# Two matmul orders and one square: the low halves last in the down projection, a later turn of half of h, and one square on VectorE

## The chip, the cores and the metric

The kernel runs on one core of one Trainium2 chip. The metric is the device time of one execution in microseconds (us). The time before is the median of three runs, 918.59 us (918.48 to 919.51). The profile is of one further execution, which took 918.14 us by the same clock and whose trace spans 916.4 us from the first to the last instruction. The core's engines are PE (TensorE: matmuls, and PEld for its weight loads), DVE (VectorE), ACT (ScalarE), POOL (GpSimd) and SP (SyncE, which issues most of the DMAs).

## The reference

A bidirectional encoder trunk of two layers over 256 tokens of width 1024, all in 32-bit floats. Cut to the sub-layers that matter here, each layer does:

```python
mixed = jax.nn.sigmoid(gate_a) * branch_a + jax.nn.sigmoid(gate_b) * branch_b
h = h + rms_norm(mixed @ w_out, g_mix_post)                       # stage "wout"

gate, up = jnp.split(rms_norm(h, g_ffn_pre) @ w_ffn_in, 2, axis=-1)   # stage "ffnin"
h = h + rms_norm((jax.nn.silu(gate) * up) @ w_ffn_out, g_ffn_post)    # down projection, "ffnout"

e = p_i @ w_ple_proj
h = h + rms_norm(jax.nn.sigmoid(h @ w_ple_gate) * e, g_ple_post)      # stage "ple"

def rms_norm(x, g):
    y = x * lax.rsqrt(jnp.mean(x * x, axis=-1, keepdims=True) + EPS)
    return y * g
```

Ahead of them in each layer stand the combined input projection, gated linear attention (branch A) and grouped-query attention (branch B). The hidden width of the feed-forward block is 2816, so its down projection multiplies 256 x 2816 by 2816 x 1024.

## The kernel before, in words

**Precision.** Each 32-bit operand of a matmul is kept as two tiles in a reduced 32-bit format: a high part (a cast by ACT) and a low part (the value minus the high part, by DVE). `split` (L133) issues this pair. A product then takes three matmuls: high x high, high x low and low x high. `mm3` (L107) issues the three for one 128 x 128 block of tokens and one 128 x 512 block of weights; `passes` (L113) does the same for several blocks, with one of the three kinds last. Weights come by DMA as 1 MB units, four blocks of 128 x 512 each, into a `raw` tile, and are split into `wh` and `wl`.

**Halves and turns.** The 256 tokens are two halves of 128 rows, `hf` 0 and 1. PE wants its left operand with the features on the partitions, so each result is turned by PE: `transpose_in` (L443) issues four 128 x 128 transposes into one accumulator (`aux`) and splits that into the high and low tiles of a `Split`. `turn_in` (L520) does so for the 1024 columns of one half, as two groups of four transposes.

**The order on PE.** Matmuls are issued in the order of the program text. Side work such as the transposes waits as a `Task`, a generator that yields how many ticks it wants to wait; `tick()` is called after about every six matmuls of 512 columns, and a task whose ticks are over is run there. `WAIT_H` (three ticks for half 0, five for half 1, both layers) is the wait of the turn of h behind the down projection; `WAIT_IN[1][1]` (six ticks) that of half 1 behind `wout` in the second layer (numbered 1; the first is numbered 0). A planner then puts each engine's instructions in order: of those that are ready by its estimate, the one of the highest priority; `tc.high_priority(AHEAD)` raises that of the norms and of the splits behind the transposes. On the chip the order is fixed, and an instruction that waits holds up all behind it on its engine.

**Down projection.** `out_step(n, hf, w)` (L1589) takes one unit of `w_ffn_out` (256 hidden features, `kk` 0 and 1, times two column halves `j`) for one half of the tokens: 12 matmuls, by `mm3` for each `kk` and `j`, into the two accumulators `o[hf][j]`. Eight of the 11 units are done between the blocks of the up projection (part `ffnin` in the tile names), and the last three in `ffnout`: all three for half 0, then all three for half 1. Behind each half follow `post_norm_add` and `turn_in(hT, ...)`:

```python
        for hf in range(2):
            for n, w in zip(outs, us):
                out_step(n, hf, w)
            ...
            post_norm_add(o[hf], gpost, hf)
            turn_in(hT, h[:, hf, :], hf, WAIT_H[l][hf])
```

`by_half(hT, after_gate, ...)` then multiplies half 0 of hT, and after it half 1, by `w_ple_gate`; the accumulators keep the name of the part in which they were made, so those of the down projection are `acc_0ffnin` and `acc_1ffnin` to the end.

**Norms.** `row_rstd` (L477) squares the parts of a row block with ACT at L495 (sums in the columns of `ss`), adds the two sums and the epsilon on POOL (L507) and takes the power -1/2 there (L511). All of its squares are written to one scratch tile, `junk`, from its first column. `post_norm_add` then multiplies by the gain (L126, DVE) and adds to h (L580, DVE, two pieces of 512 columns). `pre_norm` (L530) squares the new h, and scales it on DVE (L515, two pieces) into the tile that is turned next. `after_out` (L1507) calls both behind each half of `wout`.

Of the kernel before, what the change touches and what calls it, by code (L numbers as in the profile page):

```python
# [14 lines left out]
ALU = mybir.AluOpType  # L15
# [11 lines left out]
WAIT, WAIT_FIRST, WAIT_FFN, WAIT_BLOCK = 6, 4, 4, 6  # L27

WAIT_NEXT, WAIT_IN, WAIT_H = (7, 9), ((6, 9), (6, 6)), ((3, 5), (3, 5))
# [13 lines left out]
OUT = (0, 1, 2, 3, 4, 5, 10, 6, 7, 8, 9)  # L43
# [16 lines left out]
def trunk_kernel(ctx: ExitStack, tc: tile.TileContext, a: dict, out: bass.AP):  # L60
# [7 lines left out]
    nc = tc.nc  # L68
# [20 lines left out]
    def mid(dt=F32):  # L89
        return b4p.tile([P, 1024], dt, tag="mid", name=nm("mid"))  # L90

    def acc():
        return accp.tile([P, 512], F32, tag="acc", name=nm("acc"))

    def aux():
        return accp.tile([P, 512], F32, tag="acc", name=nm("aux"))

    def t512():
        return smp.tile([P, 512], F32, tag="t512", name=nm("t512"), bufs=5)

    def small(n, tag, bufs=None):
        return smp.tile([P, n], F32, tag=tag, name=nm(tag), **({"bufs": bufs} if bufs else {}))

    def mm(o, lhsT, rhs, start, stop):
        return nc.tensor.matmul(o, lhsT, rhs, start=start, stop=stop)  # L105

    def mm3(o, l, r, start, stop):  # L107
        (lh, ll), (rh, rl) = l, r
        mm(o, lh, rh, start, False)
        mm(o, lh, rl, False, False)  # L110
        mm(o, ll, rh, False, stop)
# [24 lines left out]
    h = cp.tile([P, 2, D], F32, tag="h", name="h")  # L136
# [69 lines left out]
    for l in range(DEPTH):  # L206
        w = a["w_in"][l]
# [12 lines left out]
        w = a["w_ffn_in"][l]  # L220
# [151 lines left out]
    def gain(v, t, n):  # L372
        nc.sync.dma_start(t[:, :n], v.unsqueeze(0).broadcast_to([P, n]))
        return t[:, :n]
# [24 lines left out]
    def tick():  # L399

        for t in list(tasks):
            t.left -= 1
            if t.left <= 0:
                t.go()
# [38 lines left out]
    def transpose_in(sp, src, k, n, hf, plain=None):  # L443

        ps = aux()
        for i in range(n):
            nc.tensor.transpose(ps[:, i * P : (i + 1) * P], src[:, i * P : (i + 1) * P], ident)
        with tc.high_priority(AHEAD):
            sp.put(ps[:, : n * P], k, n, hf * P, P)
        if plain is not None:  # L450
            nc.scalar.copy(plain, ps[:, : n * P])
# [3 lines left out]
    def in_turn():  # L455

        return tc.issue_after(last_pow[0].ins) if last_pow[0] is not None else nullcontext()
# [16 lines left out]

    last_square = [None]

    def row_rstd(parts, behind=None):  # L477

        ss, r, junk = small(3, "ss"), small(1, "rstd"), mid() if parts[0].shape[-1] > 512 else t512()
        for j, src in enumerate(parts):
            n = src.shape[-1]
            if j == 2 and behind is not None:
                last_square[0] = nc.vector.scalar_tensor_tensor(
                    out=junk[:, :n], in0=src, scalar=1.0 / 1024.0, in1=src, op0=ALU.mult, op1=ALU.mult,
                    accum_out=ss[:, j : j + 1],
                )
                nc.vector.tensor_scalar(  # L490
                    out=r, in0=ss[:, 2:3], scalar1=ss[:, 0:1], scalar2=None, op0=ALU.add
                )
            else:
                with tc.issue_after(behind.ins) if j and behind is not None else nullcontext():
                    last_square[0] = nc.scalar.activation(  # L495
                        junk[:, :n], src, AF.Square, scale=1.0 / 32.0, accum_out=ss[:, j : j + 1]
                    )
            if len(parts) == 3 and j == 1:

                with in_turn():  # L500
                    last_pow[0] = nc.gpsimd.tensor_scalar(
                        out=ss[:, 0:1], in0=ss[:, 0:1], scalar1=ss[:, 1:2], scalar2=EPS if behind is not None else 0.0,
                        op0=ALU.add, op1=ALU.add,
                    )
        with in_turn():
            if behind is None or len(parts) == 2:
                nc.gpsimd.tensor_scalar(  # L507
                    out=r, in0=ss[:, 0:1], scalar1=ss[:, len(parts) - 1 : len(parts)], scalar2=EPS,
                    op0=ALU.add, op1=ALU.add,
                )  # L510
        last_pow[0] = nc.gpsimd.tensor_tensor(out=r, in0=r, in1=neghalf[:, 0:1], op=ALU.pow)  # L511
        return r

    def scale_gain(out, in0, r, g):
        nc.vector.scalar_tensor_tensor(out=out, in0=in0, scalar=r, in1=g, op0=ALU.mult, op1=ALU.mult)  # L515

    def halves(t):
        return [t[:, j * 512 : (j + 1) * 512] for j in range(2)]

    def turn_in(sp, x, hf, wait, plain=None):  # L520


        def turn():
            yield wait
            for j, y in enumerate(halves(x)):
                transpose_in(sp, y, 4 * j, 4, hf, plain and plain[j])

        sp.makers[hf].append(Task(turn(), part[0]))

    def pre_norm(g, hf, sp, wait=WAIT, plain=None):  # L530

        x, gs = halves(h[:, hf, :]), halves(g)
        with tc.high_priority(AHEAD):
            xn = mid()
            r = row_rstd(x)
            for j, y in enumerate(halves(xn)):
                scale_gain(y, x[j], r, gs[j])

        turn_in(sp, xn, hf, wait, plain)
# [26 lines left out]
    def post_norm_add(parts, g, hf, behind=None, store=None, squared=None):  # L566

        with tc.high_priority(AHEAD):
            yt = mid()
            r = row_rstd(squared or parts, behind)  # L570
            cuts, c = [], 0
            for src in parts:
                cuts.append(slice(c, c + src.shape[-1]))
                c += src.shape[-1]
            for j, (src, c) in enumerate(zip(parts, cuts)):
                with tc.issue_after(last_square[0].ins) if j and len(parts) == 3 and behind is not None else nullcontext():
                    vmul(yt[:, c], src, g[:, c])
            for c in cuts if store else (slice(0, 512), slice(512, 1024)):
                x = h[:, hf, c]
                added = nc.vector.scalar_tensor_tensor(  # L580
                    out=x, in0=yt[:, c], scalar=r, in1=x, op0=ALU.mult, op1=ALU.add
                )
                if store:
                    store(c)
        return added
# [138 lines left out]
    def project_t(sp):  # L724

        o = [acc(), acc()]
        for kh in range(2):
            wmode(o, sp, kh * 4, ws.take(), kh == 0, kh == 1)
            ws.done()
        return o  # L730

    def project(sp):

        o = [acc(), acc()]
        for kh in range(2):
            w = ws.take()
            for hf in range(2):
                amode(o[hf], sp, hf, kh * 4, w, kh == 0, kh == 1)
            ws.done()
        return o  # L740
# [81 lines left out]
    ss = [small(2, "ss") for _ in range(2)]  # L822
# [179 lines left out]
    for l in range(DEPTH):  # L1002
# [104 lines left out]
        o = {}  # L1107
# [139 lines left out]
        for x in range(2):  # L1247
            o = project_t(uT)
            for i in range(2):
                dst = qk[:, x, 2 * i : 2 * i + 2, :]  # L1250
                src = o[i].rearrange("p (h t) -> p h t", t=T)
# [142 lines left out]
        for j in range(2):  # L1394
            o = project(uT)
# [107 lines left out]
        gpre = gain(a["g_ffn_pre"][l], mid(), D)  # L1503
        u2 = Split()
        plain = [halves(mid()) for _ in range(2)]

        def after_out(hf, o):  # L1507
            post_norm_add(o, gpost, hf)
            pre_norm(gpre, hf, u2, WAIT_IN[l][hf], plain[hf])

        if l == 0:
            embedding = embed(l, 3)
# [7 lines left out]
        hid = Split()  # L1520
# [11 lines left out]
        for hf in range(2):  # L1532
            ws.lend = hf == 1
            for b in range(2):
                o = acc()
# [51 lines left out]
        o = []  # L1587

        def out_step(n, hf, w):  # L1589
            if not o:  # L1590
                o.extend([acc(), acc()] for _ in range(2))
            wh, wl = (t[:, :2048].rearrange("p (k c) -> p k c", c=512) for t in w)
            for kk in range(2):
                k = 2 * n + kk
                hid.need(hf, k)
                for j in range(2):
                    mm3(
                        o[hf][j], hid.tok(k, hf), (wh[:, 2 * kk + j, :], wl[:, 2 * kk + j, :]),
                        n == OUT[0] and kk == 0, n == OUT[-1] and kk == 1,
                    )  # L1600
                tick()

        outs = list(OUT)
        steps, pairs, seven_ = chain.from_iterable(block(b) for b in PLAIN), list(PAIRS), None
        for x in FFN:
# [3 lines left out]
            if x == "o":  # L1609
                n, w = outs.pop(0), ws.take()  # L1610
# [16 lines left out]
        hT = Split()  # L1627
# [3 lines that stand above are left out]
                if hf == 1:  # L1631
                    ws.done()
            post_norm_add(o[hf], gpost, hf)

            turn_in(hT, h[:, hf, :], hf, WAIT_H[l][hf])


        e = big().rearrange("p (s c) -> p s c", s=2)
# [89 lines left out]
```

## Time and profile before

| what | value |
|---|---|
| time, median of 3 runs | 918.59 us (918.48 to 919.51) |
| time of the profiled execution | 918.14 us |
| its span, first to last instruction | 916.4 us |
| granted TensorE clock, mean | 0.999 |
| ACT busy in the span | 64% |
| DMA, mean over the span | 189 GB/s |

A profile here is one execution. Its page gives the busy time of each engine, a chain of work followed back from the last instruction, and groups of instructions by source line. Further views of the same trace used below are the list of waits (who waited for whom, with the total, the number and the longest in us), the chain in order of time (start, duration, what, how many), the timeline (start, duration, engine, line, operation, tile written and tiles read, count, and in brackets the idle time before it), and the instructions of one source line (durations as least/median/greatest in ns). A matmul's duration in the timeline overlaps the next one's; the distance between starts is what it costs PE.

### The profile page before, as it was taken

To read this page: it belongs to the slowest core of one execution; us is meant where nothing else is said; L and a number is where in the kernel's file an instruction comes from. 1 tells how busy PE (TensorE), PEld (TensorE's weight loads), DVE (VectorE), ACT (ScalarE), POOL (GpSimd) and SP (SyncE) were. 2 spreads that over 40 slices of the span, in tenths; PEclk is the share of its full clock that TensorE was granted. 3 is DMA by queue.
4 is the path that set the end of the run, shared out by engine and by line. 5 is a ranking of instruction groups with operands and counts; after the bars stand their busy time and mean duration, and the time that the engine had idled before them with its cause. 6 is when DMAs were issued, how large, how long until landed. Compare 5 with 4: busy or idle time off the path is not lost.

```text
span 916.4 us, 12439 instructions
## 1 busy us (share of the span) xinstructions
PE 908.1 (99%) x4674; PEld 776.5 (85%) x4674; DVE 786.2 (86%) x1007; ACT 584.1 (64%) x970; POOL 102.4 (11%) x156
## 2 busy tenths in 40 slices
PE   9999999999999999999999999999999999999996
PEld 8998888888888888888899988888888888888886
DVE  6989989987669998999779789799876899989885
ACT  6688767564567565566676687675645766565563
POOL 3700221300100000000334001110001000000000
PEclk9999999999999999999999999999999999999999
DMA  8664445657385555657576424455574756555361
GB/s 283 199 202 136 139 138 190 213 186 255 107 302 181 200 199 199 232 168 247 178 260 222 147 92 139 138 184 184 184 252 134 269 172 211 222 172 222 122 246 46
DMA packets 88680, 173.45 MB, mean 189 GB/s; under 512 B 3422, under 2 KB 26470, under 8 KB 88108
## 3 DMA queue, kind: packets, MB, share of 16 engines
q1 hardware_dynamic: 88316, 172.27, 55.3%
q8 instruction: 36, 0.59, 0.3%
q10 hardware_dynamic: 304, 0.40, 0.1%
q14 instruction: 24, 0.20, 0.1%
HBM read 169.50 MB, written 3.15 MB: 188 GB/s over the span
## 4 chain that ended last, share of the span: by engine, by line
PE 96%; DVE 2%; issue 1%; ACT 0%; POOLq 0%; POOL 0%; DVEq 0%; ACTq 0%
PE acc_1ffnin L121 12%; PE acc_0ffnin L121 11%; PE acc_1gate L121 7%; PE acc_0gate L121 7%; PE acc_1ffnin L105 7%; PE acc_0ffnin L105 6%; PE acc_1rq L121 3%; PE acc_0gqk L121 3%; PE acc_1gqk L121 3%; PE acc_1wout L121 2%; PE acc_0wout L121 2%; PE acc_0ple L121 2%; PE acc_1gg L121 2%; PE acc_0gg L121 2%; PE acc_1v L121 2%; PE acc_0v L121 2%
## 5 line engine op out<-in xcount | busy, mean ns | idle before, releaser
L105 PE MATMUL acc_0ffnin<-wh_0ffnin,big_0ffnin 128*128 128x512 f32 x176 | 56.9, 393 | 0.1
L105 PE MATMUL acc_1ffnin<-wh_1ffnin,big_1ffnin 128*128 128x512 f32 x176 | 56.8, 392 | 0.0
L133 ACT CAST wh_1ffnin<-raw_1ffnin 128x1024 fp32r<-128x1024 f32 x38 | 38.5, 1049 | 26.8 <-DMA raw_1ffnin<-in_w_ffn_out_dram 8.6
L133 ACT CAST wh_0ffnin<-raw_0ffnin 128x1024 fp32r<-128x1024 f32 x38 | 38.2, 1048 | 24.8 <-PE acc_0ffnin L121 7.1
L133 DVE TENSOR_TENSOR wl_1ffnin<-raw_1ffnin,wh_1ffnin 128x1024 fp32r<-128x1024 f32 x38 | 44.9, 1220 | 8.7 <-ACT wh_1ffnin L133 8.6
L133 DVE TENSOR_TENSOR wl_0ffnin<-raw_0ffnin,wh_0ffnin 128x1024 fp32r<-128x1024 f32 x38 | 44.7, 1220 | 8.3 <-ACT wh_0ffnin L133 8.1
L121 PE MATMUL acc_1ffnin<-wh_1ffnin,big_1wout 128*128 128x512 f32 x168 | 42.5, 393 | 0.0
L121 PE MATMUL acc_0ffnin<-wh_0ffnin,big_0wout 128*128 128x512 f32 x168 | 42.5, 393 | 0.0
L105 PEld LDWEIGHTS acc_0ffnin<-wh_0ffnin,big_0ffnin 128*128 128x128 f32 x176 | 33.0, 188 | 7.2 <-DVE big_0ffnin L133 0.5
L105 PEld LDWEIGHTS acc_1ffnin<-wh_1ffnin,big_1ffnin 128*128 128x128 f32 x176 | 33.1, 188 | 6.7
L133 DVE TENSOR_TENSOR wl_1ffnin<-lent_1ffnin,wh_1ffnin 128x1024 fp32r<-128x1024 f32 x30 | 35.8, 1218 | 1.8 <-ACT wh_1ffnin L133 1.7
L133 DVE TENSOR_TENSOR wl_0ffnin<-lent_0ffnin,wh_0ffnin 128x1024 fp32r<-128x1024 f32 x30 | 35.8, 1217 | 1.7 <-ACT wh_0ffnin L133 1.7
L121 PEld LDWEIGHTS acc_0ffnin<-wh_0ffnin,big_0wout 128*128 128x128 f32 x168 | 31.1, 188 | 6.2
L121 PEld LDWEIGHTS acc_1ffnin<-wh_1ffnin,big_1wout 128*128 128x128 f32 x168 | 31.1, 188 | 6.2
L133 ACT CAST wh_1ffnin<-lent_1ffnin 128x1024 fp32r<-128x1024 f32 x30 | 30.7, 1052 | 8.0 <-PE acc_1ffnin L105 3.9
L133 ACT CAST wh_0ffnin<-lent_0ffnin 128x1024 fp32r<-128x1024 f32 x30 | 30.7, 1053 | 7.5 <-PE acc_0ffnin L105 3.9
L105 PE MATMUL acc_1ffnin<-wl_1ffnin,big_1ffnin 128*128 128x512 f32 x88 | 34.3, 389 | 0.0
L105 PE MATMUL acc_0ffnin<-wl_0ffnin,big_0ffnin 128*128 128x512 f32 x88 | 34.3, 389 | 0.0
L133 DVE TENSOR_TENSOR wl_1gate<-raw_1gate,wh_1gate 128x1024 fp32r<-128x1024 f32 x20 | 23.5, 1219 | 7.8 <-ACT wh_1gate L133 7.7
L133 ACT CAST wh_1gate<-raw_1gate 128x1024 fp32r<-128x1024 f32 x20 | 19.9, 1049 | 16.0 <-DMA raw_1gate<-in_w_o_attn_dram 7.0
L133 ACT CAST wh_0gate<-raw_0gate 128x1024 fp32r<-128x1024 f32 x20 | 19.9, 1047 | 14.2 <-DMA raw_0gate<-in_w_o_attn_dram 6.3
L133 DVE TENSOR_TENSOR wl_0gate<-raw_0gate,wh_0gate 128x1024 fp32r<-128x1024 f32 x20 | 24.2, 1257 | 5.4 <-ACT wh_0gate L133 5.3
(720 smaller groups left out, 2715.7 us busy)
## 6 DMA issues: line engine op xcount, KB each, us to landing
raw_0ffnin<-in_w_ffn_out_dram SPq DMA_DIRECT2D x11, 1024.0 KB, 5.8
raw_1ffnin<-in_w_ffn_out_dram SPq DMA_DIRECT2D x11, 1024.0 KB, 5.4
lent_0ffnin<-in_w_ffn_in_dram SPq DMA_DIRECT2D x6, 1024.0 KB, 7.5
lent_1ffnin<-in_w_ffn_in_dram SPq DMA_DIRECT2D x6, 1024.0 KB, 6.8
raw_0v<-in_w_in_dram SPq DMA_DIRECT2D x4, 1024.0 KB, 5.0
raw_0gate<-in_w_o_gla_dram SPq DMA_DIRECT2D x4, 1024.0 KB, 5.1
raw_0gate<-in_w_o_attn_dram SPq DMA_DIRECT2D x4, 1024.0 KB, 5.4
raw_0wout<-in_w_ffn_in_dram SPq DMA_DIRECT2D x8, 512.0 KB, 5.1
```

What stands on the lines that cost most here:

```text
L105: return nc.tensor.matmul(o, lhsT, rhs, start=start, stop=stop)
L121: nc.tensor.matmul(o, x, y, start=start and n == 0, stop=stop and n == len(seq) - 1, **kw)
L133: return nc.scalar.copy(hi, src), nc.vector.tensor_tensor(out=lo, in0=src, in1=hi.bitcast(F32), op=ALU.subtract)
```

## The change

Three edits. **First**, `out_step` no longer goes through `mm3` block by block. For one unit it issues the four high x high products (both `kk`, both `j`), then the four high x low products, then the four low x high products. It issues 12 matmuls as before, and its two ticks lie behind the sixth and the twelfth, as before. **Second**, `turn_in` has a flag `apart` that puts one more tick between its two groups of four transposes; it is set for the turn of half 0 of h behind the down projection, in both layers. **Third**, `row_rstd` has a flag `here`, with which its second square is a multiply with a running sum on DVE in place of ACT's; `pre_norm` hands it on, and it is set behind `wout` in the second layer, for half 1.

```diff
-    def row_rstd(parts, behind=None):
+    def row_rstd(parts, behind=None, here=False):
...
+            elif j == 1 and here:
+                nc.vector.scalar_tensor_tensor(
+                    out=junk[:, :n], in0=src, scalar=1.0 / 1024.0, in1=src, op0=ALU.mult, op1=ALU.mult,
+                    accum_out=ss[:, 1:2],
+                )
             else:
                 with tc.issue_after(behind.ins) if j and behind is not None else nullcontext():
...
-    def turn_in(sp, x, hf, wait, plain=None):
+    def turn_in(sp, x, hf, wait, plain=None, apart=False):
         def turn():
             yield wait
             for j, y in enumerate(halves(x)):
+                if j and apart:
+                    yield 1
                 transpose_in(sp, y, 4 * j, 4, hf, plain and plain[j])
...
-    def pre_norm(g, hf, sp, wait=WAIT, plain=None):
+    def pre_norm(g, hf, sp, wait=WAIT, plain=None, here=False):
...
-            r = row_rstd(x)
+            r = row_rstd(x, here=here)
...
-            pre_norm(gpre, hf, u2, WAIT_IN[l][hf], plain[hf])
+            pre_norm(gpre, hf, u2, WAIT_IN[l][hf], plain[hf], here=l == 1 and hf == 1)
...
             for kk in range(2):
-                k = 2 * n + kk
-                hid.need(hf, k)
-                for j in range(2):
-                    mm3(
-                        o[hf][j], hid.tok(k, hf), (wh[:, 2 * kk + j, :], wl[:, 2 * kk + j, :]),
-                        n == OUT[0] and kk == 0, n == OUT[-1] and kk == 1,
-                    )
-                tick()
+                hid.need(hf, 2 * n + kk)
+            for p in range(3):
+                for kk in range(2):
+                    hi, lo = hid.tok(2 * n + kk, hf)
+                    for j in range(2):
+                        x, w = ((hi, wh), (hi, wl), (lo, wh))[p]
+                        mm(
+                            o[hf][j], x, w[:, 2 * kk + j, :],
+                            n == OUT[0] and kk + p == 0, n == OUT[-1] and kk + p == 3,
+                        )
+                    if p == 1 + kk:
+                        tick()
...
-            turn_in(hT, h[:, hf, :], hf, WAIT_H[l][hf])
+            turn_in(hT, h[:, hf, :], hf, WAIT_H[l][hf], apart=hf == 0)
```

## The prediction

> **What bounds the kernel now.** First I read the page's busy times and its chain of waits.
>
> ```profile
> span 916.4 us, 12439 instructions
> ```
>
> ```profile
> PE 908.1 (99%) x4674; PEld 776.5 (85%) x4674; DVE 786.2 (86%) x1007; ACT 584.1 (64%) x970; POOL 102.4 (11%) x156
> ```
>
> ```profile
> PE 96%; DVE 2%; issue 1%; ACT 0%; POOLq 0%; POOL 0%; DVEq 0%; ACTq 0%
> ```
>
> TensorE is the bound: it is busy for 908.1 of 916.4 us and holds 96% of the chain. The change removes no matmul, so it can save only time in which PE waits. The second view is the list of waits of PE's weight loads, where a late operand shows first.
>
> ```profile
> PEld acc_0ffnin L105 <- DVE big_0ffnin L133: 0.5, 1, 0.5
> ```
>
> ```profile
> PEld aux_0ffnout L447 <- DVE h L580: 0.4, 2, 0.2
> PEld aux_1wout L447 <- DVE mid_1wout L515: 0.3, 1, 0.3
> ```
>
> ```profile
> PEld aux_1wout L447 <- PE aux_1wout L447: 0.3, 1, 0.3
> ```
>
> Each edit meets one of these places: the low half of a hidden tile (0.5 us, first layer only), the transposes of h (0.4 us, first layer only), and those behind the second layer's wout (0.3 and 0.3 us). These are idle times of the weight loads, which run ahead of the matmuls; what PE loses is less, and is read from the starts of matmuls. For that I need PE's undisturbed step, from the chain in order of time.
>
> ```profile
> 10.08 3.08 PE acc_0rq L105 x19
> ```
>
> ```profile
> 149.70 1.75 PE aux_0gg L447 x16
> ```
>
> ```profile
> 483.00 5.82 PE acc_1rq L121 x36
> ```
>
> ```profile
> 843.67 5.44 PE acc_1ffnin L105 x24
> ```
>
> A matmul of 512 columns in the down projection costs 5.44/24 = 0.227 us, a transpose 1.75/16 = 0.109. So six matmuls, one tick, are 1.36 us.
>
> **Edit 1, the low halves last.** The first layer's wait in the timeline: the tile's high half on ACT, its low half on DVE, and PE.
>
> ```profile
> 417.83 0.59 ACT L133 CAST big_0ffnin<-aux_0ffnin 128x512 fp32r<-128x512 f32 x1 [1.84 <-PE aux_0ffnin L447]
> ```
>
> ```profile
> 418.99 0.68 DVE L133 TENSOR_TENSOR big_0ffnin<-aux_0ffnin,big_0ffnin 128x512 fp32r<-128x512 f32 x1
> ```
>
> ```profile
> 419.02 0.39 PE L105 MATMUL acc_0ffnin<-wh_0ffnin,big_0ffnin 128*128 128x512 f32 x1
> 419.25 0.39 PE L105 MATMUL acc_0ffnin<-wl_0ffnin,big_0ffnin 128*128 128x512 f32 x1
> 419.72 0.73 PE L105 MATMUL acc_0ffnin<-wh_0ffnin,big_0ffnin 128*128 128x512 f32 x2
> 420.30 0.39 PE L105 MATMUL acc_0ffnin<-wl_0ffnin,big_0ffnin 128*128 128x512 f32 x1
> ```
>
> The unit begins at 419.02. Its third matmul, the first with a low half, starts at 419.72, 0.47 behind the second: 0.25 too late, because DVE ends the low half at 418.99 + 0.68 = 419.67. From there to 420.30 two steps take 0.58, another 0.12 over. In the new order the low half is wanted behind eight matmuls, at 419.02 + 8 x 0.227 = 420.84, 1.17 us after it is there; the high half is done at 418.42 and does not limit. The edit takes away **0.37 us**. In the second layer the list has no such wait, so nothing. The three kinds for one unit remain 12 matmuls at 0.227, and both ticks stand behind the same counts, so no transpose moves. `o[hf][0]` now ends one matmul before `o[hf][1]` instead of three, 0.45 us later. What hides this is in the next rows.
>
> **Does the saved time stay?** Behind half 0 of the down projection comes the turn of h, three ticks later. PE at the end of half 0, ACT there, DVE's two additions to h, and PE's transposes:
>
> ```profile
> 425.09 0.62 PE L105 MATMUL acc_0ffnin<-wh_0ffnin,big_0ffnin 128*128 128x512 f32 x2
> ```
>
> ```profile
> 423.95 2.00 ACT L133 CAST wh_0ffnin<-raw_0ffnin 128x1024 fp32r<-128x1024 f32 x2 [0.60 <-DMA raw_0ffnin<-in_w_ple_gate_dram]
> 425.85 0.59 ACT L495 ACTIVATE t_0ffnout<-acc_0ffnin 128x512 f32<-128x512 f32 x1
> ```
>
> ```profile
> 428.50 1.41 DVE L580 SCALAR_TENSOR_TENSOR h<-mid_0ffnout,rstd_0ffnout,h 128x512 f32<-128x512 f32 x2
> ```
>
> ```profile
> 418.50 0.37 SPq L297 DMA_DIRECT2D raw_0ffnin<-in_w_ple_gate_dram  x1
> ```
>
> ```profile
> 429.40 1.22 PE L447 MATMUL aux_0ffnout<-ident,h 128*128 128x128 f32 x8
> ```
>
> ```profile
> 429.96 0.42 PEld L447 LDWEIGHTS aux_0ffnout<-ident,h 128*128 128x128 f32 x4 [0.20 <-DVE h L580]
> ```
>
> The last matmul of half 0 starts at 425.09 and ends 0.39 later, at 425.48, but ACT squares only at 425.85, behind two weight casts, which wait for a DMA issued at 418.50, before PE's wait. So a later `o[0][0]` costs nothing, and an earlier PE does not bring h forward either: I keep its second piece's end at 428.50 + 1.41 = 429.91, and the first's at about 428.50 + 0.74 = 429.24 (one such instruction alone is the 0.74 of L580 below). PE, 0.37 earlier, reaches the first group of transposes at 429.40 - 0.37 = 429.03. The second group starts 0.05 behind its data (429.91 to 429.96); by the same 0.05 the first can start at 429.29, so PE waits 0.26 there. Of the 0.37, **0.11 stays**.
>
> **Edit 2, the second group a tick later.** Without waits it would follow the first at 429.40 + 4 x 0.109 = 429.84; it starts at 429.96. The wait of 0.12 goes, since a tick of 1.36 us lies between: **-0.12**. Nothing is late next, by these rows: the moved group's high half on ACT and low half on DVE go behind other work in their queues, but columns 512 to 1023 are first used in the ple stage after 24 matmuls:
>
> ```profile
> 434.73 8.39 PE acc_0ple L121 x37
> ```
>
> That is 434.73 + 24 x 0.227 = 440.2, some 9 us after the new place of the transposes. The moved step issues no DMA. The second layer's eight:
>
> ```profile
> 881.19 1.08 PE L447 MATMUL aux_1ffnout<-ident,h 128*128 128x128 f32 x8
> ```
>
> They take 1.08 against the first layer's 1.22, so a wait of 0.12 isn't there to save. Each layer gets one more change between matmuls and transposes. Around the hidden tile's transposes,
>
> ```profile
> 417.20 0.60 PE L447 MATMUL aux_0ffnin<-ident,t_0ffnin 128*128 128x128 f32 x4
> ```
>
> four transposes and seven matmuls (those from 417.55 to 418.78) lie before 419.25: 2.05 us, against 4 x 0.109 + 7 x 0.227 = 2.03. So a change costs some 0.02; with nothing removed it can't gain. For both layers I take **+0.05**, at most 0.1.
>
> **Edit 3, one square on DVE.** The second layer's wout, by engine: DVE, ACT, POOL, PE.
>
> ```profile
> 710.80 0.74 DVE L580 SCALAR_TENSOR_TENSOR h<-mid_1wout,rstd_1wout,h 128x512 f32<-128x512 f32 x1
> 711.46 2.35 DVE L133 TENSOR_TENSOR wl_1wout<-raw_1wout,wh_1wout 128x1024 fp32r<-128x1024 f32 x2
> 714.66 1.41 DVE L515 SCALAR_TENSOR_TENSOR mid_1wout<-h,rstd_1wout,mid_1wout 128x512 f32<-128x512 f32 x2 [0.84 <-POOL rstd_1wout L511]
> 715.99 1.22 DVE L133 TENSOR_TENSOR wl_1wout<-raw_1wout,wh_1wout 128x1024 fp32r<-128x1024 f32 x1
> ```
>
> ```profile
> 711.85 0.63 ACT L495 ACTIVATE t_1wout<-h 128x512 f32<-128x512 f32 x1
> 712.38 0.19 ACT L495 ACTIVATION_READ_ACCUMULATOR t_1wout<-h 128x1 f32 x1
> 712.60 0.64 ACT L495 ACTIVATE t_1wout<-h 128x512 f32<-128x512 f32 x1
> 713.14 0.18 ACT L495 ACTIVATION_READ_ACCUMULATOR t_1wout<-h 128x1 f32 x1
> ```
>
> ```profile
> 713.42 0.56 POOL L507 TENSOR_SCALAR rstd_1wout<-ss_1wout 128x1 f32<-128x1 f32 x1 [3.33 <-ACT t_1wout L495]
> ```
>
> ```profile
> 714.49 1.07 PE L121 MATMUL acc_1ffnin<-wl_1wout,big_1wout 128*128 128x512 f32 x4
> 715.46 0.66 PE L447 MATMUL aux_1wout<-ident,mid_1wout 128*128 128x128 f32 x4
> ```
>
> Without waits the first group would begin at 714.49 + 4 x 0.227 = 715.40 and the second at 715.84. The first begins 0.06 late; the second can't before DVE's second piece ends, at 714.66 + 1.41 = 716.07, 0.23 late, to which the loading of its first block adds a little: some 0.3 us in all, as the list has it. If both squares ran side by side this would go. But they can't: `row_rstd` gives both squares the same columns of `junk`, so DVE's square, which writes there, must wait until ACT's has ended, at 712.38 + 0.19 = 712.57. That is when ACT's own second square begins today (712.60). The duration of the new one, by the nearest rows of such an instruction, is 0.74 for 512 columns (L580) with a read of its sum behind it:
>
> ```profile
> L596 DVE SCALAR_TENSOR_TENSOR mid_1ple<-mid_1ple x1: 424/424/424, 907.4 to 907.4; 128x256 f32<-128x256 f32 x1
> L596 DVE DVE_READ_ACCUMULATOR mid_1ple<-mid_1ple x1: 81/81/81, 907.7 to 907.7; 128x1 f32 x1
> ```
>
> So the sum is there at 712.61 + 0.74 + some 0.05 = 713.40 against 713.14 + 0.18 = 713.32 on ACT. I take **+0.1** for the delay of POOL and of both groups. The bounds are -0.3 (the wait is gone) and the rival below. [...]
>
> The second low half of `wl_1wout` is queued behind the square: from 713.4 to 714.6. PE wants it with the third of the four `wl` matmuls, at 714.49 + 0.45 = 714.94, so 0.3 us are left. ACT is freed of 0.72 us, which nobody waits for.
>
> **Sum**, against the profiled execution's own 918.14 us: -0.11 - 0.12 + 0.05 + 0.1 = -0.08. That execution lies 0.45 below the median of the runs, 918.59, so I forecast 918.59 - 0.08, **918.5**, for the median: no change. A difference of 0.2%, 1.84 us, is about what a measurement of this kernel can tell.
>
> **Rivals.** *The square comes behind both low halves* (slower). ACT's square ends at 712.57; DVE's first low half lets go at 711.46 + 2.35 - 1.22 = 712.59. The planner takes what is ready, and a tie of 0.02 us decides: if by its estimate the square is not ready there, the second low half goes first, to 713.81, the square starts at 713.74, POOL at 714.60 in place of 713.42, and both groups of transposes come 1.18 us later, with nothing to fill PE. With the other terms: 918.14 - 0.18 + 1.18 = 919.1, or 919.6 for the median. A third unit's low half (now at 715.99) taken ahead of the two L515 pieces would cost about as much, a DVE subtraction of 1.2 less the wait for POOL. For it speaks that DVE is full there and ACT is not; against it, the square's raised priority. [...]
>
> *All the waits go* (faster): -0.37 - 0.12 - 0.3 + 0.05 = -0.74, 917.8 for the median. For it, the waits are real and on the chain; against it, the fixed time of h and the shared `junk`. More than this isn't there: 1.84 us would need twice all of these waits.
>
> *Changing accumulators costs* (slower): each matmul now writes another accumulator than the one before. At 5 ns, for 12 matmuls in each of 11 units, two halves and two layers, 528 in all, it is 2.6 us, 921.1. Against it: the first layer's `rq_first` (L105) changes its accumulator with every matmul and takes 3.08/19 = 0.162 us, the second layer's `rq_step` (L121), with six on one, 5.82/36 = 0.162, both on 288 and 384 columns.
>
> **How the numbers follow.** Forecast 0.45; the late square 0.25; all waits gone 0.13; accumulators 0.04; an order of the planner that these rows don't show, elsewhere, 0.13. Faster by over 0.2% could only come from the last: 0.05. Slower by over 0.2%: accumulators 0.04, half of the last, and some 0.06 of the late square, where a second wait follows it: 0.17. The remaining 0.78 is within 0.2%. The range runs from 917.6, the fast rival with 0.2 for the bound of edit 2 and the spread of the runs, to 920.2, the slow one with 0.5 for a nanosecond on each changed accumulator and a little for the same spread.
>
> **What would show it.** Right: no wait for `big_0ffnin` in PE's list, a new one of about 0.26 us for the first piece of h at the first layer's turn and none for the second, the down projection still at 0.227 a matmul, and POOL's L507 in the second layer's wout about 0.1 us later behind DVE. Wrong: DVE's square starting before ACT's has ended, `mid_1wout` (L515) a microsecond late behind low halves, a down projection above 0.227, or waits at places that the change doesn't touch.

## The result, and the profile after

The changed kernel takes 924.04 us (median of 6 runs, 922.91 to 925.98) against 918.54 for the kernel before (6 runs): a ratio of 1.006, interval 1.005 to 1.007. It is 5.5 us slower, by more than the 0.2% that a measurement can tell, and above the forecast range. The profiled execution took 924.25 us, against 918.14 before. The page of the changed kernel, with the span, PE and DVE in the span, and the chain of waits by engine:

```profile
span 922.2 us, 12435 instructions
...
PE 909.7 (99%) x4674; PEld 777.5 (84%) x4674; DVE 787.5 (85%) x1009; ACT 583.5 (63%) x968; POOL 103.0 (11%) x156
...
PE 88%; DVE 4%; DMA 2%; issue 2%; POOL 2%; ACT 1%; POOLq 0%; SPq 0%; DVEq 0%; ACTq 0%
```

The work has hardly grown, but the chain now leaves PE for a DMA, for DVE and for POOL. The list of waits of PE's weight loads in the changed kernel (total, number, longest in us):

```profile
PEld aux_1emb L982 <- DMA mid_0ffnout<-in_p_dram: 2.3, 1, 2.3
PEld acc_1rq L121 <- DVE wl_0ple L133: 1.4, 1, 1.4
...
PEld aux_1wout L447 <- DVE mid_1wout L520: 1.0, 1, 1.0
...
PEld aux_0ffnout L447 <- DVE h L587: 0.3, 1, 0.3
```

The last row is the one that was forecast for h, and the forecast absence of `big_0ffnin` holds too. The first two rows were in no list before: a wait for p, the input of the second layer's embedding, which is turned in the first layer's ple stage; and one for weights' low halves at the second layer's start. To see what each costs, take the start of the same matmul in both traces, after less before, as the distance grows (+0.17 us at the start of the two executions):

| us in the trace before | after less before | step |
|---|---|---|
| 300 | +0.17 | start |
| 432 to 440 | -0.28 | -0.45: -0.38 by 426, edit 1; the rest at the turn of h |
| 446 to 455 | +3.51 | +3.79: p and what follows it |
| 460 | +3.74 | +0.23 |
| 474 to 600 | +5.21 | +1.47: start of the second layer |
| 711 | +5.15 | -0.06 |
| 716 to the end | +5.79 | +0.64: edit 3 |

**The wait for p.** PE's timeline of the changed kernel:

```profile
444.26 1.07 PE L121 MATMUL acc_0ple<-wl_0ffnout,big_0ffnout 128*128 128x512 f32 x4
447.18 0.88 PE L982 MATMUL aux_1emb<-ident,mid_0ffnout 128*128 128x128 f32 x4 [1.85 <-DMA mid_0ffnout<-in_p_dram]
447.85 1.91 PE L447 MATMUL aux_0ffnout<-ident,h 128*128 128x128 f32 x8
449.58 0.79 PE L121 MATMUL acc_0ple<-wh_0ffnin,big_0ffnout 128*128 128x512 f32 x1
450.18 0.63 PE L121 MATMUL acc_0ple<-wl_0ffnin,big_0ffnout 128*128 128x512 f32 x1
```

The four transposes of p (`embed`) stand in PE's queue ahead of the transposes of half 1 and of the products that need these, and p is not there. Half 1 of h is: DVE's additions to it started at 437.69 and took 1.40 us, so it was there at 439.09, and its transposes start only at 447.85, behind those of p. The reason is in SyncE's queue. Its timeline before,

```profile
436.47 0.46 SPq L967 DMA_DIRECT2D mid_0ffnout<-in_p_dram  x1
...
441.25 0.37 SPq L297 DMA_DIRECT2D raw_0ffnout<-in_w_in_dram  x1
```

and after:

```profile
441.39 0.37 SPq L297 DMA_DIRECT2D raw_0ffnout<-in_w_in_dram  x1
441.81 1.15 SPq L974 DMA_DIRECT2D mid_0ffnout<-in_p_dram  x1
```

The load of `w_in` needs a `raw` buffer, which comes free at 441, when DVE ends the last low half out of it (441.22 before, 441.36 after). Before, p was issued ahead of it and was there when PE turned it at 443.0, 6.5 us after its issue. Now it stands behind the load: issued 5.3 us later, and used from 447.18, as soon as it is there.

**The slow clock and the late low halves.** Windows of the kernel before (PE, PEld, DVE, ACT and POOL busy, granted clock, DMA share, GB/s):

```profile
444.00:447.00 3.00, 3.00 (x16) 2.52 (x15) 1.89 (x3) 2.97 (x6) 0.00 (x0) 1.00 0.57 231
447.00:449.00 2.00, 2.00 (x10) 1.67 (x9) 1.90 (x4) 1.72 (x5) 0.00 (x0) 1.00 0.00 0
449.00:451.00 2.00, 2.00 (x16) 1.88 (x16) 1.15 (x2) 1.36 (x3) 0.93 (x2) 1.00 0.00 0
...
471.00:473.00 2.00, 2.00 (x14) 2.00 (x14) 2.00 (x3) 1.45 (x3) 2.00 (x2) 1.00 0.92 249
```

and of the changed one:

```profile
444.00:447.00 3.00, 1.33 (x6) 0.75 (x4) 0.00 (x0) 0.00 (x0) 0.00 (x0) 1.00 1.04 398
447.00:449.00 2.00, 1.82 (x10) 1.83 (x11) 0.29 (x1) 0.64 (x2) 0.00 (x0) 0.62 0.40 162
449.00:451.00 2.00, 2.00 (x8) 1.55 (x7) 1.68 (x3) 1.72 (x3) 0.00 (x0) 0.53 0.00 0
...
471.00:473.00 2.00, 0.78 (x7) 0.55 (x5) 2.00 (x4) 2.00 (x5) 1.13 (x1) 1.00 0.57 238
```

Two things follow the wait. In this execution the granted clock falls to 0.62 and 0.53, so the transposes of h start 0.22 us apart (447.85 to 449.58, eight) in place of 0.109; 2.0 us of the 3.79 are the wait (444.26 + 4 x 0.227 = 445.17 to 447.18), and the other 1.8 are lost in the slow stretch. Not all of the 1.8 is the clock's: with edit 2 alone (below) the same stretch loses 0.6 at full clock, most of it in a wait for ACT's `big_0ffnout`.

And from 444 to 447 DVE and ACT have nothing to do (0.00 us, against 1.89 and 2.97 before). Their work comes later, and in another order. The low half of `wl_0ple` that PE lacks at 471.7 was made at 462.96 before, ahead of the additions to h:

```profile
462.96 1.25 DVE L133 TENSOR_TENSOR wl_0ple<-raw_0ple,wh_0ple 128x1056 fp32r<-128x1056 f32 x1
464.99 1.41 DVE L580 SCALAR_TENSOR_TENSOR h<-mid_0ple,rstd_0ple,h 128x512 f32<-128x512 f32 x2 [0.78 <-POOL rstd_0ple L511]
```

Now it is the first of the three at 471.68, behind the additions, and these wait for POOL:

```profile
463.46 4.43 POOL L568 TENSOR_SCALAR em_0ple<-he_0ple 128x1 f32<-128x1 f32 x1
```

```profile
469.15 1.42 DVE L587 SCALAR_TENSOR_TENSOR h<-mid_0ple,rstd_0ple,h 128x512 f32<-128x512 f32 x2 [1.34 <-POOL rstd_0ple L516]
470.48 1.29 DVE L126 TENSOR_TENSOR mid_0ple<-h,mid_0ple 128x512 f32<-128x512 f32 x2
471.68 3.60 DVE L133 TENSOR_TENSOR wl_0ple<-raw_0ple,wh_0ple 128x1056 fp32r<-128x1056 f32 x3
```

DVE works without a break from 457.95 to 467.81. One POOL instruction of one column takes 4.43 us beside it and ends at 467.89; what `rstd` still needs follows, and DVE stands idle for 1.34 us. The high half that it is made from was there at 466.1 (ACT). So I read the wait for `wl_0ple` as the new order of DVE's queue together with the long POOL instruction.

**Edit 3.** DVE and POOL behind the second layer's wout, in the changed kernel:

```profile
717.76 0.68 DVE L494 SCALAR_TENSOR_TENSOR t_1wout<-h 128x512 f32<-128x512 f32 x1
718.37 0.08 DVE L494 DVE_READ_ACCUMULATOR t_1wout<-h 128x1 f32 x1
718.37 1.22 DVE L133 TENSOR_TENSOR wl_1wout<-raw_1wout,wh_1wout 128x1024 fp32r<-128x1024 f32 x1
```

```profile
718.55 1.21 POOL L512 TENSOR_SCALAR rstd_1wout<-ss_1wout 128x1 f32<-128x1 f32 x1 [3.29 <-DVE t_1wout L494]
719.85 0.56 POOL L516 TENSOR_TENSOR rstd_1wout<-rstd_1wout,neghalf 128x1 f32<-128x1 f32 x1
```

The square comes in time, between the two low halves. But POOL's add of one column (L507 before, L512 now) takes 1.21 us and not 0.56, and ends at 719.76, 0.17 behind the low half that DVE started meanwhile (718.37 + 1.22 = 719.59).

### The profile page after: what moved, and what is told of

It reads as the page before. It is cut to its first block, busy times and chain, and to the rows that moved or that the text cites. A ratio compares the mean times of both kernels' runs of the same rounds, so it can differ in the third digit from the quotient of the medians.

```text
span 922.2 us, 12435 instructions
## 1 busy us (share of the span) xinstructions
PE 909.7 (99%) x4674; PEld 777.5 (84%) x4674; DVE 787.5 (85%) x1009; ACT 583.5 (63%) x968; POOL 103.0 (11%) x156
## 4 chain that ended last, share of the span: by engine, by line
PE 88%; DVE 4%; DMA 2%; issue 2%; POOL 2%; ACT 1%; POOLq 0%; SPq 0%; DVEq 0%; ACTq 0%
PE acc_1ffnin L121 11%; PE acc_0ffnin L121 11%; PE acc_0gate L121 7%; PE acc_1gate L121 7%; PE acc_1ffnin L105 7%; PE acc_0ffnin L105 4%; PE acc_1gqk L121 2%; PE acc_0gqk L121 2%; PE acc_0wout L121 2%; PE acc_1gg L121 2%; PE acc_0gg L121 2%; PE acc_1v L121 2%; PE acc_0v L121 2%; PE acc_1merge L121 2%; PE acc_0merge L121 2%; PE acc_1rq L121 2%
## 5 line engine op out<-in xcount | busy, mean ns | idle before, releaser
L105 PE MATMUL acc_1ffnin<-wh_1ffnin,big_1ffnin 128*128 128x512 f32 x176 | 45.4, 391 | 0.0
L105 PE MATMUL acc_0ffnin<-wh_0ffnin,big_0ffnin 128*128 128x512 f32 x176 | 45.4, 391 | 0.0
L105 PE MATMUL acc_1ffnin<-wl_1ffnin,big_1ffnin 128*128 128x512 f32 x88 | 24.6, 394 | 0.0
L105 PE MATMUL acc_0ffnin<-wl_0ffnin,big_0ffnin 128*128 128x512 f32 x88 | 24.6, 393 | 0.0
```

## The experiments

My theory: edit 2 moves p in the queue, which costs 4.9 us of the 5.5; edit 3 costs 0.6 because GpSimd's add, 1.21 us in place of 0.56, stands still while VectorE subtracts; edit 1 does no harm. The rivals: the new order of products moves the ticks; or the later half of h upsets the ple stage by itself, and p only shows it. Before is 918.41 us (25 runs) beside the first four kernels, 918.62 (21) beside the next four and 918.24 (27) beside the last three.

**Edit 1 alone** (`out_step` as changed; `turn_in` and `row_rstd` as before).

> Edit 1 alone: the kernel before with the down projection's new order of products, h turned in one go, ScalarE squaring. Theory (the loss comes from edit 2, whose tick turns round two transfers in SyncE's queue): the wait of 0.4 us for a low half at 419.7 is gone, the transfer of p stays ahead of the load of w_in, so 918.2 to 918.6, no difference from before. Rival (the order of products itself costs, through the ticks that it moves): slower, up to the whole 5.5 us.

917.76 us, ratio 0.9991 (0.9982 to 1.0000). p's issue stays ahead of the load, no wait for it appears, and the rival falls. From 422 us on its matmuls start 0.38 us earlier than before, counted from the start, and stay so. The median is 0.4 below the expected range, inside what can't be told.

**Edit 2 alone.**

```diff
-            turn_in(hT, h[:, hf, :], hf, WAIT_H[l][hf])
+            turn_in(hT, h[:, hf, :], hf, WAIT_H[l][hf], apart=hf == 0)
```

> Edit 2 alone: the kernel before with the second half of h turned a tick later. Theory: here the transfer of p stands behind the load of w_in, TensorE waits some 2 us for p near 447 and runs at about half its clock until 451, and the next layer starts late by 1.4 us: 3.9 to 5.4 us slower, 922.4 to 924.0. Rival (a joint effect of edits 1 and 2): within 0.5 us of before.

923.59 us, 1.0064 (1.0043 to 1.0085), a time as the theory said. One tick alone turns the two issues round. Its waits, and its windows:

```profile
PEld aux_1emb L982 <- DMA mid_0ffnout<-in_p_dram: 2.8, 1, 2.8
...
PEld acc_1rq L121 <- DVE wl_0ple L133: 1.4, 1, 1.4
```

```profile
447.00:449.00 2.00, 1.17 (x11) 1.17 (x12) 0.00 (x0) 0.48 (x1) 0.00 (x0) 1.00 0.31 122
449.00:451.00 2.00, 1.71 (x10) 1.25 (x9) 1.86 (x3) 1.98 (x4) 0.00 (x0) 1.00 0.00 0
```

Here PE waits longer for p than in the changed kernel, yet the clock stays at 1.00. The wait goes with the edit, the slow clock only with some executions.

**Edit 3 alone** (`here=l == 1 and hf == 1`, nothing else).

> Edit 3 alone: the kernel before with VectorE squaring the second half in the second layer. Theory (GpSimd's add of the two halves of the sum stands still while VectorE runs its two-input operations back to back): TensorE's transposes at 714 come 0.6 us later, 919.1 to 919.3. Rival, the prediction's own count (the add's duration is fixed at 0.56 us): 0.1 us later, 918.6.

919.46 us, 1.0011 (1.0002 to 1.0021), 1.05 over before and 0.2 above the expected range. In its trace the matmuls start 0.08 us later than before at 711 and 0.71 from 716 on, a step of 0.63; the rest of the difference is inside what can't be told. DVE and POOL:

```profile
713.30 1.22 DVE L133 TENSOR_TENSOR wl_1wout<-raw_1wout,wh_1wout 128x1024 fp32r<-128x1024 f32 x1
```

```profile
713.48 1.21 POOL L512 TENSOR_SCALAR rstd_1wout<-ss_1wout 128x1 f32<-128x1 f32 x1 [3.29 <-DVE t_1wout L494]
```

The add starts about where the prediction had it and takes twice as long; the prediction's 0.1 falls. Why the add is long, the held low half below tells.

**All edits, p issued first.** `embed` gets p's tile from outside; its DMA is issued behind the load of the gain.

```diff
         gple = gain(a["g_ple_post"][l], mid(), D)
+        pin = load_p(l + 1) if l + 1 < DEPTH else None
...
-            embedding = embed(l + 1, 3)
+            embedding = embed(l + 1, 3, pin)
```

> The changed kernel with the transfer of p issued right behind the load of the gain, ahead of the queue of weight loads. Theory: with p early, the wait of 2.0 us at 447 and the slow clock behind it are gone, and of the 5.5 us only edit 3's 0.6 and what the order of VectorE's work costs at the next layer's start (0 to 1.4) stay: 918.7 to 920.3. Rival (the loss comes from the reordered work of VectorE and GpSimd in this stage, the late p being a bystander): 922 or more.

918.99 us, 1.0011 (1.0002 to 1.0020): 5.05 of the 5.5 us are gone, the waits for p and for `wl_0ple` and the slow clock with them. What stays by the medians, 0.58, is about edit 3's 0.6:

```profile
PEld aux_1wout L447 <- DVE mid_1wout L520: 0.9, 1, 0.9
```

**The kernel before, p issued late.** Nothing of the change is in it.

```diff
-        nc.sync.dma_start(pin, a["p"][l, 0].rearrange("(s p) c -> p s c", p=P))
+        with tc.issue_after(ws.issued.ins) if l else nullcontext():
+            nc.sync.dma_start(pin, a["p"][l, 0].rearrange("(s p) c -> p s c", p=P))
```

Here `ws.issued` is the last load of weights that was issued.

> The kernel before, with nothing changed but that the transfer of p for the second layer is issued behind the load of w_in in SyncE's queue, as in the changed kernel. Theory (the place of p in the queue is the whole cause of edit 2's loss): TensorE waits 2.0 to 2.5 us for p near 445 and again some 1.4 us near 473, 922.3 to 923.9. Rival (the later second half of h does part of the harm itself, by moving the work of VectorE and GpSimd behind it): at most 921.

923.02 us, 1.0046 (1.0031 to 1.0060): 4.4 over before, where edit 2 alone had 5.2, with intervals that overlap. The place of this one transfer makes the loss, as far as can be told, and both waits, without the later turn:

```profile
PEld aux_1emb L976 <- DMA mid_0ffnout<-in_p_dram: 2.8, 1, 2.8
PEld acc_1rq L121 <- DVE wl_0ple L133: 1.4, 1, 1.4
```

```profile
463.50 4.44 POOL L561 TENSOR_SCALAR em_0ple<-he_0ple 128x1 f32<-128x1 f32 x1
```

The second wait is thus no separate effect of the later turn: it comes with the late p, and so does the long POOL instruction. But p is not all that the planner moved here. From 436 us on, through the ple stage, every queue of this kernel has the order of edit 2 alone, in which PE turns p eleven products later than before and DVE makes that low half behind the additions. What this order costs and what p's lateness costs by itself, no run separates.

**The changed kernel, PE filled.**

```diff
             ps = aux()
+            if l:
+                for _ in range(7):
+                    mm(ps, hT.tok(0, 0)[0], hT.at(0, 4, 0, P)[0], True, True)
```

> The changed kernel with seven further products of 512 columns (1.6 us, their result overwritten and used by nothing) on TensorE just ahead of the transposes of p, where it waits. Theory A (the clock that fell to 0.53 to 0.62 at 447 to 451 answers to the idle time and costs up to 1.8 us): the clock stays at 1.0, 922.2 to 923.3. Theory B (the clock does not answer to the idle time, or its cost is covered by later waits): as the changed kernel, 924.0; slower by up to 1.6 if p comes sooner than 1.6 us after the wait begins.

922.51 us, 1.0049 (1.0032 to 1.0067), 1.5 under the changed kernel. But it did not run as planned: the planner put the seven products at 438.21, and further products of the gate and the transposes of half 1 ahead of p's.

```profile
438.21 1.75 PE L105 MATMUL aux_1emb<-big_0ffnout 128*128 128x512 f32 x7
```

```profile
446.95 0.66 PE L985 MATMUL aux_1emb<-ident,mid_0ffnout 128*128 128x128 f32 x4
```

```profile
447.00:449.00 2.00, 2.00 (x11) 1.75 (x12) 0.69 (x1) 1.34 (x2) 0.00 (x0) 1.00 0.16 66
449.00:451.00 2.00, 2.00 (x11) 1.64 (x11) 0.82 (x2) 1.72 (x4) 0.00 (x0) 1.00 0.00 0
```

With no idle PE the clock stays at 1.00, as theory A has it, but the time can't be held against it: the order changed too, the seven products themselves take 1.6 us of PE, and the interval overlaps the changed kernel's. Edit 2 alone kept its clock without any filling. Theory A is not settled by it. What it does show: with other work ahead of p's transposes, a late p costs PE next to nothing at that place (its weight loads wait 0.4 us). The wait for `wl_0ple` comes all the same (1.2 us in two pieces), so it is no echo of PE's idle time at 447.

**Edit 3, the low half held back.** The second low half of the unit is made behind the gain (L515) in place of ahead of it.

```diff
-                    self.last[n] = split(*piece)
+                    if n == 132 and j == 1:
+                        hi, lo, src = piece
+                        nc.scalar.copy(hi, src)
+                        self.late = lambda hi=hi, lo=lo, src=src: vsub(lo, src, hi.bitcast(F32))
+                    else:
+                        self.last[n] = split(*piece)
...
+            if hf and part[0] == "1wout":
+                with tc.issue_after(last.ins):
+                    ws.late()
```

> Edit 3 alone, with the second low half of the weights that VectorE makes between the square and the gain put behind the gain. Theory (GpSimd's add stands still while VectorE runs a two-input subtraction out of SBUF): the add takes 0.30 us and not 1.21, the transposes start 0.2 us before those of the kernel before, 918.1 to 918.4 if the low half is not then late for TensorE. Rival (the add is long since one of its two sums comes from VectorE): the add stays at 1.2 us, 919.2.

920.60 us, 1.0028 (1.0017 to 1.0039). The time is a miss, the mechanism a hit:

```profile
713.38 0.30 POOL L517 TENSOR_SCALAR rstd_1wout<-ss_1wout 128x1 f32<-128x1 f32 x1 [3.29 <-DVE t_1wout L499]
```

```profile
716.96 0.73 PE L121 MATMUL acc_1ffnin<-wl_1wout,big_1wout 128*128 128x512 f32 x2 [1.88 <-DVE wl_1wout L129]
```

The sum still comes from DVE and the add takes 0.30 us, so the rival falls. But the condition of the forecast, a low half in time, was not met: it ends at 716.9, and PE stands still ahead of it.

**Edit 1 with the same low half held back**, ScalarE squaring.

> Edit 1 alone, with the same low half put behind the gain, ScalarE squaring both halves. Theory: the add takes 0.30 us in place of 0.56 and the transposes at 714 start 0.26 us sooner than in low_last_only, 917.5. Rival (the low half, made some 3 us later, is then late for TensorE): 917.8 to 919.

919.42 us, 1.0015 (1.0005 to 1.0025), slower as the rival said, and 0.4 above its range. The add takes 0.30 here too, and PE waits for the same low half:

```profile
PEld acc_1ffnin L121 <- DVE wl_1wout L129: 2.3, 1, 2.3
```

In the kernel before, too, this add lost 0.26 us to the low half beside it. Made behind the gain, though, the low half is late.

**What the edits are worth with the queue kept.** p's DMA is issued just ahead of the last load of the down projection's stage; edits 1 and 2, edit 2 alone, and once more edit 1 alone.

```diff
                 if hf == 1:
+                    if l + 1 < DEPTH and n == outs[-1]:
+                        pin = load_p(l + 1)
                     ws.done()
```

> Edits 1 and 2 without edit 3, with the transfer of p issued ahead of the weight loads of the ple stage. Theory: the waits at 447 and 473 do not appear, edit 1 brings 0.38 us, edit 2 itself 0.1 to 0.2, and the low half at 714 stays as before: 917.6 to 918.0 beside 918.4 to 918.6 of before. Rival (edit 2 hurts the ple stage by more than the queue): 918.5 or more.

> Edit 2 alone with the transfer of p issued ahead of the weight loads of the ple stage. Theory: 0.1 to 0.2 us faster than before, 918.2 to 918.5, with no wait for p. Rival: the later half of h delays the gate's products, 918.8 or more.

> The kernel of low_last_only once more, beside the other two on one chip, to see whether edit 1 alone beats the kernel before: 917.8 to 918.1, 0.4 to 0.6 us under before. Rival: no difference that can be told.

917.85 us, 0.9998 (0.9989 to 1.0007); 917.96, 1.0001 (0.9992 to 1.0010); 917.84, 0.9999 (0.9990 to 1.0008). There is no wait for p in any of them; edits 1 and 2 with p first turn it at 438.3:

```profile
L988 PE MATMUL aux_1emb<-ident,mid_0ffnout x4: 270/272/272, 438.3 to 438.6; 128*128 128x128 f32 x4
```

Medians lie 0.3 to 0.4 below before and the traces show PE earlier from 446 to 600, by 0.1 us (edit 2), 0.5 (both) and 0.4 and 0.5 (edit 1, its two traces), but the intervals hold 1.0. The trace of edit 3 alone is 0.2 earlier there, too, with nothing of edits 1 and 2 in it, so edit 2's 0.1 is not its own. The two rivals that foresaw harm fall; the third, that edit 1 makes no difference that can be told, stands. A gain is not shown. No version tried beats the kernel before by more than can be told; edits 1 and 2 with p first are 6 us faster than the changed kernel.

## Why the prediction was wrong

**The step that failed** is edit 2: "Nothing is late next, by these rows" and "The moved step issues no DMA". Both are true of the moved transposes themselves. But with a tick more the planner ordered the work behind it anew, and two DMAs of other steps, p and a load of `w_in`, changed places in SyncE's queue. Forecast -0.12 us; measured +4.9 in the trace of edit 2 alone, and in the changed kernel's +3.79, +0.23 and +1.47, which is 5.5, or 5.0 less the gain of 0.45 ahead of them. The forecast had this as "an order of the planner that these rows don't show, elsewhere", with 0.13 and no price. A part of the price could be had: the trace before shows p issued 4.8 us ahead of a load that waits for its buffer, and used 6.5 us after its issue. Issued behind that load, at 441.6 or later, it had to be late for a use at 443.0. The 1.4 us of the second wait could not be read from those rows.

**Edit 1** removed what it was to remove (0.37 forecast; 0.38 in its trace), the low half's wait is gone, and a matmul still takes 0.227 us. "Of the 0.37, 0.11 stays" was too little. The prediction took h's time from one execution and held it fixed, and in that execution h was late. ACT's casts ahead of h's squares start at 423.95 there, when the DMA that they wait for has landed. With edit 3 alone, which changes nothing in this stage, they start earlier:

```profile
423.72 2.00 ACT L133 CAST wh_0ffnin<-raw_0ffnin 128x1024 fp32r<-128x1024 f32 x2
```

That trace runs 0.34 us behind the one before up to here, so the casts come 0.57 earlier by the same count. In the kernel before with p late they come 0.64 earlier, with edit 1 alone 0.42 and 0.60 (two traces). The landing thus moves from one execution to the next, and not by the edit. Against the trace before, 0.36 and 0.54 of edit 1's gain are left from 446 to 600; against that of edit 3 alone, which gains 0.2 in the same place, 0.15 and 0.33. The wait of PE's weight loads for h was 0.3 as forecast, yet it cost PE almost nothing: in the changed kernel the two products ahead start at 428.73, which with 2 x 0.227 gives 429.18, and the first transpose starts at 429.21. The load for these products was issued at 428.50, 0.23 ahead, so an idle load is not an idle PE.

**Edit 2 in its own place**: -0.12 forecast, -0.1 in the trace with p first, but this is no sign that the term was right. Between 426 and 440 edit 3 alone gains 0.19 and the kernel before with p late 0.17, without edit 2: the 0.12 between the two groups of transposes was h's lateness in the one execution that was read. The extra changes between matmuls and transposes were too small to see.

**Edit 3**: the square itself was forecast well, with its start behind ACT's sum and 0.68 us against 0.74. The term that was mis-sized is POOL's add: taken as a fixed 0.56, so +0.1; measured 1.21, so +0.64. In the trace before it stood beside a low half of DVE which ended at 713.81, and it ended at 713.98. The same line at other places of the kernel before took from 0.29 to 1.39 us (least/median/greatest in ns):

```profile
L507 POOL TENSOR_SCALAR rstd_0wout<-ss_0wout x4: 289/302/702, 239.0 to 257.2; 128x1 f32<-128x1 f32 x4
L507 POOL TENSOR_SCALAR rstd_0ple<-ss_0ple x2: 363/878/1394, 449.4 to 462.9; 128x1 f32<-128x1 f32 x2
```

One of the short ones:

```profile
427.35 0.30 POOL L507 TENSOR_SCALAR rstd_0ffnout<-ss_0ffnout 128x1 f32<-128x1 f32 x1 [96.93 <-ACT t_0ffnout L495]
```

**The rivals.** The late square did not happen: it went between the low halves. All waits gone was wrong, since edit 3 lengthened one. Changing accumulators cost nothing that shows, by edit 1 alone (917.76 us against 918.41, and still 0.227 a matmul); the 5 ns of this rival was the author's supposition, which no row or run shows. Of the signs named as wrong, `mid_1wout` came 0.6 us late (edit 3 alone), by way of POOL's add beside a low half and not because the square went behind one; and the last one came, waits at places that the change doesn't touch. The other two stayed away.

**Open**: why the clock fell in the changed kernel's execution, after 2.0 us of idle PE, and not after 2.5 and 2.6 us in two others; and what the planner's new order costs apart from p's lateness.

## What to carry to other kernels

Where a planner orders the queues, a step moved by one tick can turn round DMA issues that have nothing to do with it: list the issues around it, note which stand next to one that waits for a buffer, and price the swap. A small transfer that is wanted early belongs ahead of loads that wait, and pinned there. The length of a small GpSimd instruction is no constant (0.29 to 1.39 us for one line here): look at what VectorE runs beside it, and compare the same line at another place. And a wait of 0.1 or 0.2 us read from one execution can be that execution's alone: here a DMA that landed half a microsecond late made the price of two terms.

## What the hardware did that was not expected

GpSimd's add of one column takes 0.30 us with VectorE idle, and beside VectorE's subtraction it ended 0.17 us after that: 0.56 and 1.21 us in the kernels before and after, 0.30 in both kernels with the low half held back. The instruction of 4.43 us near 463 ran beside VectorE's work without a break. Not all of VectorE's work lengthens the add: that of 0.30 us at 427.35 ran beside multiplications (L126):

```profile
427.31 1.28 DVE L126 TENSOR_TENSOR mid_0ffnout<-acc_0ffnin,mid_0ffnin 128x512 f32<-128x512 f32 x2
```

These read an accumulator and a tile, the subtraction the tiles `raw` and `wh`. Whether that makes the difference, no run shows.

The granted clock fell to 0.53 after an idle time of 2.0 us in one execution and stayed at 1.00 after 2.5 and 2.6 us in two others. Shorter windows of the changed kernel, three of them here, show half the clock from 447.5 to 450.9 us, for 3.4 us:

```profile
447.00:448.00 1.00, 0.82 (x5) 0.83 (x6) 0.00 (x0) 0.00 (x0) 0.00 (x0) 0.74 0.79 320
448.00:449.00 1.00, 1.00 (x7) 1.00 (x6) 0.29 (x1) 0.64 (x2) 0.00 (x0) 0.50 0.01 4
450.00:451.00 1.00, 1.00 (x4) 0.77 (x4) 0.84 (x2) 0.98 (x2) 0.00 (x0) 0.56 0.00 0
```

In the clock records of that trace the clock falls at 447.473 and rises at 450.886. TensorE had been idle from 445.17 to 447.18 there; in the two others, from 445.31 to 447.83 (edit 2 alone) and from 445.59 to 448.16 (before, p late), the idle time was longer and the clock stood at 1.00 from 440 to 455. So its length alone does not decide in these three executions, and what does, no run shows.
